# A hybrid block with two RWKV directions: the backward one put in reversed time, and triangles turned through DRAM

## The chip, the cores and the metric

The kernel runs on one core of one Trainium2 chip. The metric is the device time of one execution in microseconds (us). A core has five engines with a queue each: TensorE (PE in the profile; PEld is its loading of weights), VectorE (DVE), ScalarE (ACT), GpSimd (POOL) and SyncE (SP), which issues all of this kernel's DMAs.

## The reference

One layer of a block on 512 latent tokens and 256 context tokens of width 1024, all in f32: a projection of the normalized input into three branches (RWKV-7, convolution, mLSTM) and gates, the gated merge of the three, and an MLP. The change touches the RWKV branch alone. It has 8 heads of 64, and each of two directions runs a recurrence over the context and then over the latents; the second one runs backward in time over each:

```python
def step(S, inp):
    w_t, k_t, v_t, kk_t, a_t = inp[:5]
    S = (S * w_t[:, :, None, :]
         - jnp.einsum('bhvk,bhk->bhv', S, kk_t)[..., None] * (kk_t * a_t)[:, :, None, :]
         + v_t[..., None] * k_t[:, :, None, :])
    y = jnp.einsum('bhvk,bhk->bhv', S, inp[5]) if emit else None
    return S, y
...
for d in range(2):
    rev = d == 1
    w_c, k_c, a_c = fc[4][d]
    s_ctx, yc = _rwkv7_scan(s0, w_c, k_c, fc[2], fc[3], a_c, fc[0], rev, emit_ctx)
    w_l, k_l, a_l = fl[4][d]
    _, yl = _rwkv7_scan(s_ctx, w_l, k_l, fl[2], fl[3], a_l, fl[0], rev, True)
    y_lat = y_lat + yl
```

Decay `w` and rate `a` are the direction's own; `r`, `k`, `v` and `kk` are the same for both. The two outputs are added, normalized by head and gated.

## The kernel before, in words

Matrices lie with features on the 128 partitions and time along the free axis: 512 latent columns, then 256 of context. Dense products take every weight as a high and a low half (`whalf`, L147: a DMA of raw weights, a ScalarE copy that rounds, a POOL subtraction), three products each. The stages follow one another in program order:

- Normalization and modulation, then the feature stage: the first half of the convolution, and for the RWKV branch `shifted` (L302, a dense product and the token shift), `normalize`, `operands` (L326) and `values` (L410). `operands` works on one head and both directions at once, the forward one on partitions 0 to 63, the backward one on 64 to 127: it loads keys into `BK` and `r` into `rd` for both halves, scans the log decay within chunks of 64 (L352 forward, L353 backward with reversed operands), takes exponentials, multiplies, and stores `al` and `bk` to DRAM. `values` transposes `v` on TensorE and stores it.
- The mLSTM stage (`front` and `back` of four heads). In the middle of it stands `rw.run(rw.ctx(0), rw.lat(0))` (L482), which prepares the first pair of RWKV heads.
- Four weaves (`weave`, L1142), one for each pair of heads. A weave runs `chain(j)` (L1085): twelve chunks one after another, in each of them a product with the state (L1100), a product with the inverted triangle (L1106, operand `LT`), and the state's update (L1115 on TensorE, L1116 on VectorE). The two directions visit the chunks in different orders (`ORDER`), with their own PSUM tiles `ch0` and `ch1`, one buffer each; `u` of both goes to the lower half of `UV`, and is copied again into `UU` (L1119), from where `output` (L1072) makes one product for both directions. Between the chain's thirds (36 in a weave) the weave places other work, so much for each third by `PACE` (preparation of the next pair) and `DENSE` (products of gates and projections, some 120 in a weave); `paced` lets it issue only behind the chain's last instruction. The tail of the pair before (norm, gate) stands there too.
- Preparation of a pair is `ctx` (L922) and `lat` (L936): `gram` (L954) makes the chunks' products on TensorE and VectorE writes them masked into `LT` (L976), `LR` (L978) and the other half of `AL` (L984); `transposed` (L987) turns the keys on TensorE; `invert` (L1002) inverts the 64x64 triangles of 24 chunks. For that, VectorE transposes four blocks of 32 partitions from `LT` into `N` (L1012), so that partitions are chunks; 30 recurrence steps of two ops each (L1017, L1019) invert 32x32 triangles; two transposes make `TN` (L1022, L1024) and four take N back into `LT` (L1042); TensorE makes the off-diagonal blocks (L1033, L1034, L1048, L1049), which ScalarE copies out.
- The merge of the branches and the MLP.

The order on an engine's queue is set ahead of the run by a planner that simulates the program and takes what is ready by priority; the chain's instructions have the highest.

Of the kernel before, what the change touches and what calls it, by code (L numbers as in the profile page):

```python
# [17 lines left out]
P = 128  # L18
# [30 lines left out]
CONST_ORDER = [("ident", 128), ("bones", 128), ("gmf", 128), ("gmb", 128), ("nmf", 128), ("nmb", 128)]  # L49
# [27 lines left out]
def build(tc, wblk, wada, xin, cin, params, lora, consts, rowp, out, dbg=None):  # L77
# [45 lines left out]
    for j in range(4):  # L123
# [5 lines left out]
        sp["v", j] = DR.tile([T, P], F32, name=f"sp_v{j}")  # L129
# [164 lines left out]
    for i in range(2):  # L294
        z, y = SO.tile([P, 752], F32, name=f"z{i}"), SO.tile([P, NT], F32, name=f"cy{i}")
        gated(i, z[:, :])
        tiles.append((i, z[:, :], y[:, :]))
# [20 lines left out]
    G.memset(mk[0:64, :, 0:1], 0.0)  # L318
    G.memset(mk[64:128, :, CH - 1:CH], 0.0)

    Es = [(SO.tile([P, T], F32, name=f"E{i}"), SO.tile([P, NCH, CH], F32, name=f"Ep{i}")) for i in range(2)]
    for _, Ep in Es:
        G.memset(Ep[0:64, :, 0:1], 1.0)
        G.memset(Ep[64:128, :, CH - 1:CH], 1.0)

    def operands(j, h, kb, r):  # L326

# [27 lines left out]
        A.activation(Ep[0:64, :, 1:CH], ct[0:64, :, 0:CH - 1], AF.Exp, scale=-0.5 * RALPHA)  # L355
        A.activation(Ep[64:128, :, 0:CH - 1], ct[64:128, :, 1:CH], AF.Exp, scale=-0.5 * RALPHA)
# [5 lines left out]
        for d in range(2):  # L362
            G.tensor_copy(PL[HF[d], j, :, h:h + 1], E3[HF[d], :, CH - 1:CH] if d == 0 else E3[HF[d], :, 0:1])
# [13 lines left out]
    A.activation(wdt[:, :], t, AF.Tanh)  # L377
    t = shifted(13, True, "vj", 2)
    V.tensor_copy(adt[:, :], t)
# [30 lines left out]
    def values(j, rk):  # L410
        vj = shifted(8 + j, True, "vj", 2)
        for c2 in range(2):
            pt = PS1.tile([P, 3, P], F32, tag="tp", name="tp", bufs=1)
            for i in range(3):
                PE.transpose(pt[:, i, :], vj[:, (c2 * 3 + i) * P:(c2 * 3 + i + 1) * P], ident)
            vt = S1.tile([P, 3, P], F32, tag="vt", name="vt", bufs=2)
            A.copy(vt[:, :, :], pt[:, :, :])
            SY.dma_start(sp["v", j][c2 * 384:c2 * 384 + 384, :].rearrange("(c t) v -> t c v", t=P), vt[:, :, :])
# [7 lines left out]
    for j in range(4):  # L426
# [5 lines left out]
        rks.append(rk)  # L432
        for h in range(2):
            operands(j, h, kbs[j], rj)
# [429 lines left out]
PACE = [4] * 8 + [3] * 8 + [2] * 12 + [0] * 8  # L864
# [4 lines left out]
class Rwkv:  # L869
    ORDER = [[8, 9, 10, 11, 0, 1, 2, 3, 4, 5, 6, 7], [11, 10, 9, 8, 7, 6, 5, 4, 3, 2, 1, 0]]  # L870
# [7 lines left out]
    def pair_set(self, i, S):  # L878
        if i == 0:
            self.BK = [S.tile([P, NCH, 2, CH], F32, name=f"BK{h}") for h in range(2)]  # L880
        self.LT.append(S.tile([P, 32, CH], F32, name=f"LT{i}"))
        self.tc.nc.gpsimd.memset(self.LT[i][:, 24:32, :], 0.0)
        for h in range(2):
            for d in range(2):
                self.AL[d].append(S.tile([P, 20, CH], F32, name=f"AL{d}{i}{h}"))
            self.LR.append(S.tile([P, 8, CH], F32, name=f"LR{i}{h}"))
        if i == 0:
            self.tmp = S.tile([P, 256], F32, name="tmp")
            self.N = S.tile([P, 32, 32], F32, name="N")
            self.TN = S.tile([P, 32, 32], F32, name="TN")  # L890
# [3 lines left out]
    def open_a(self):  # L894
# [3 lines left out]
        self.PS, self.PG = PS, [PS]  # L898
        self.AL, self.LR, self.LT, self.BKt = [[], []], [], [], []
# [589 lines left out]
```

## Time and profile before

| | us |
|---|---|
| three runs | 1367.76, 1372.55, 1374.81 |
| median | 1372.55 |
| the profiled execution | 1377.12 |
| its span, first to last instruction | 1375.3 |
| TensorE matmul busy in it | 1252.9 (91%) |
| TensorE weight load busy | 969.6 (71%) |
| VectorE busy | 849.2 (62%) |
| POOL busy | 585.7 (43%) |
| ScalarE busy | 511.8 (37%) |

All stages below are read from the profiled execution, in us from the first instruction on. The stages of interest are the feature stage (its RWKV heads stand at about 160 to 272 us), the mLSTM (to 541.9) and the weaves, which begin at 541.9, 620.6, 708.4 and 796.7 us. Busy shares are means over stages of different kinds, so the rows are asked for by stretch. A matmul's busy time overlaps that of the next one. In an f32 product the records come in twos.

### The profile page before, as it was taken

How to read it: one execution, taken by the hardware profiler on the slowest of the kernel's cores; microseconds unless marked ns; L12 is line 12 of the kernel's file. 1: busy time of each engine (PE TensorE's matmuls, PEld its weight loads, DVE VectorE, ACT ScalarE, POOL GpSimd, SP SyncE). 2: the span in 40 equal slices, each digit the busy share in tenths (PEclk: the TensorE clock that was granted, in tenths of full speed). 3: DMA queues.
4: the chain of work that ended last, by engine and by line, in shares of the span. 5: the costliest groups of instructions: out<-in, count | busy, mean ns of one | idle time of the engine just before them, and what ended most of it. 6: DMA issues, size and time to landing. Idle time of an engine off the chain costs nothing.

```text
span 1375.3 us, 21700 instructions
## 1 busy us (share of the span) xinstructions
PE 1252.9 (91%) x8004; PEld 969.6 (71%) x8004; DVE 849.2 (62%) x1509; ACT 511.8 (37%) x1048; POOL 585.7 (43%) x547
## 2 busy tenths in 40 slices
PE   6999989786999886999899988889999999999997
PEld 1587877565888775667566665667888878888886
DVE  2599588889266993797977857678366534300202
ACT  4434556632222231243342444422354444322322
POOL 0443334426755441332433435533456544444442
PEclk9999999898999997999998998999999999999999
DMA  9221588732633314323431244787434433433422
GB/s 375 65 69 58 134 270 255 246 104 62 186 99 97 111 64 120 110 93 101 143 110 49 85 145 136 259 263 249 131 112 156 142 100 95 153 104 96 131 95 89
DMA packets 101457, 187.85 MB, mean 137 GB/s; under 512 B 10708, under 2 KB 29396, under 8 KB 100328
## 3 DMA queue, kind: packets, MB, share of 16 engines
q1 hardware_dynamic: 101352, 186.47, 42.9%
q8 instruction: 63, 1.03, 0.3%
q14 instruction: 42, 0.34, 0.1%
HBM read 148.64 MB, written 29.40 MB: 129 GB/s over the span
## 4 chain that ended last, share of the span: by engine, by line
PE 45%; DVE 14%; DMA 5%; issue 3%; ACT 1%; POOL 1%; SPq 0%; DVEq 0%; POOLq 0%; ACTq 0%
PE pt L1268 16%; PE pd L1337 13%; PE dg L512 5%; DMA wad<-wada 4%; DVE N L1019 3%; DVE tmp L1017 2%; PE pg L973 2%; PE ch L1100 1%; PE pd L682 1%; DVE N L1012 1%; PE ch L1106 1%; DVE accm L608 1%; PE dl L262 1%; PE pbk L998 1%; PE ch L1115 1%
## 5 line engine op out<-in xcount | busy, mean ns | idle before, releaser
L153 POOL TENSOR_TENSOR wlo<-raw,whi 128x512 fp32r<-128x512 f32 x296 | 435.5, 1477 | 555.5 <-ACT whi L152 488.9
L152 ACT CAST whi<-raw 128x512 fp32r<-128x512 f32 x296 | 182.0, 618 | 318.7 <-PE pt L1268 118.8
L262 PE MATMUL dl<-hh,wlo 128*128 128x512 f32 (+1 forms) x368 | 149.7, 407 | 10.8 <-POOL wlo L153 10.8
L262 PE MATMUL dl<-hh,whi 128*128 128x512 f32 (+1 forms) x368 | 151.4, 412 | 2.7 <-ACT kT L758 1.9
L262 PE MATMUL dl<-hl,whi 128*128 128x512 f32 (+1 forms) x368 | 148.5, 403 | 0.0
L1337 PE MATMUL pd<-h2l,whi 128*128 128x512 f32 (+1 forms) x272 | 103.3, 381 | 0.7 <-POOL h2l L1320 0.7
L1337 PE MATMUL pd<-h2h,wlo 128*128 128x512 f32 (+1 forms) x272 | 102.7, 379 | 0.0
L1337 PE MATMUL pd<-h2h,whi 128*128 128x512 f32 (+1 forms) x272 | 101.5, 380 | 0.2 <-ACT h2h L1317 0.2
L1363 DVE TENSOR_TENSOR x<-pt,modb 128x512 f32<-128x512 f32 x8 | 5.5, 690 | 154.7 <-PE pt L1268 154.7
L1268 PE MATMUL pt<-whi,h1h 128*128 128x512 f32 x256 | 99.6, 389 | 0.0
L1268 PE MATMUL pt<-whi,h1l 128*128 128x512 f32 x256 | 99.6, 389 | 0.0
L1268 PE MATMUL pt<-wlo,h1h 128*128 128x512 f32 x256 | 99.1, 389 | 0.0
L262 PEld LDWEIGHTS dl<-hh,wlo 128*128 128x128 f32 (+1 forms) x368 | 70.7, 192 | 26.0 <-POOL wlo L153 11.2
L262 PEld LDWEIGHTS dl<-hh,whi 128*128 128x128 f32 (+1 forms) x368 | 71.2, 193 | 18.6 <-ACT kT L758 2.1
L262 PEld LDWEIGHTS dl<-hl,whi 128*128 128x128 f32 (+1 forms) x368 | 70.8, 192 | 15.2 <-issue 1.5
L608 DVE SCALAR_TENSOR_TENSOR accm<-wad,sc,accm 128x512 f32<-128x512 f32 x56 | 59.1, 1056 | 35.2 <-DMA wad<-wada 34.6
L1113 POOL TENSOR_TENSOR sps<-SV,PL 64x128 f32<-64x128 f32 x88 | 40.0, 454 | 85.1 <-DVE SV L1116 81.9
L1341 DVE TENSOR_TENSOR relu<-relu 128x512 f32<-128x512 f32 x32 | 38.9, 1218 | 55.8 <-ACT relu L1340 55.7
L512 PE MATMUL dg<-hl,whi 128*128 128x512 f32 x144 | 66.5, 462 | 0.0
L512 PE MATMUL dg<-hh,whi 128*128 128x512 f32 x144 | 65.7, 456 | 0.0
L512 PE MATMUL dg<-hh,wlo 128*128 128x512 f32 x144 | 65.6, 456 | 0.0
L1019 DVE TENSOR_TENSOR N<-N,tmp 128x30 f32<-128x30 f32 (+14 forms) x120 | 58.1, 484 | 3.0
(389 smaller groups left out, 2792.3 us busy)
## 6 DMA issues: line engine op xcount, KB each, us to landing
raw<-wblk SPq DMA_DIRECT2D x296, 256.0 KB, 2.9
wad<-wada SPq DMA_DIRECT2D x64, 256.0 KB, 4.0
wada<-wada SPq DMA_DIRECT2D x8, 1024.0 KB, 13.4
BK<-kb SPq DMA_DIRECT2D x16, 384.0 KB, 5.2
sp_bk<-BK SPq DMA_DIRECT2D x8, 768.0 KB, 5.2
BK<-sp_bk SPq DMA_DIRECT2D x8, 768.0 KB, 4.1
sp_g<-gt SPq DMA_DIRECT2D x24, 256.0 KB, 2.0
sp_al<-al SPq DMA_DIRECT2D x8, 640.0 KB, 4.6
```

Source lines behind the costliest of these rows:

```text
L152: A.copy(hi[:, :], raw[:, :])
L153: G.tensor_tensor(lo[:, :], raw[:, :], hi[:, :], ALU.subtract)
L262: PE.matmul(ps_[0:M, :], lhsT=w[:, ko:ko + M], rhs=x[seg][:, k, :], start=(n == 0), stop=(n == 3 * KT - 1))
L512: yield lambda w=w, x=x, k=k, ko=ko, n=n: PE.matmul(ps[:, :], lhsT=w[:, ko:ko + P], rhs=x[:, k, :], start=(n == 0), stop=(n == 3 * KT - 1))
L608: V.scalar_tensor_tensor(o, t[:, :], sc[:, k, 0:1], o, ALU.mult, ALU.add)
L973: PE.matmul(ps[hf, i, :, :], lhsT=BK[dd, c, x, :], rhs=al[:, c] if lat else AL[d][dd, 8 + c:9 + c, :], start=True, stop=True)
L1017: V.tensor_tensor(tv, N[:, s + 1:32, s:s + 1].to_broadcast([P, n, s]), N[:, s:s + 1, 0:s].to_broadcast([P, n, s]), ALU.mult)
L1019: V.tensor_tensor(N[:, s + 1:32, 0:s], N[:, s + 1:32, 0:s], tv, ALU.add)
L1113: last["Pool"] = G.tensor_tensor(sps[hf], SV[d][hf, c, :, :], PL[hf, c, :].unsqueeze(2).to_broadcast([64, 2, CH]), ALU.mult)
L1268: PE.matmul(pss[i][:, :], lhsT=x[:, k, ts_], rhs=w[:, :], start=(k == 0 and n == 0), stop=(k == nk - 1 and n == 2))
L1337: PE.matmul(ps[:, ts_], lhsT=w[:, ko:ko + P], rhs=x[:, k, ts_], start=(k == 0 and n == 0), stop=(k == 7 and n == 2))
L1341: V.tensor_tensor(t[:, :], t[:, :], t[:, :], ALU.mult)
```

## The change

The backward direction's operands are turned round in time as they are made (each of the two segments for itself), so that in every later step it looks like the forward one.

- Feature stage: reversed copies of keys (`kr`), of `r` (`rr`) and of `v` (`vr`) on POOL, reversed writes of the two low-rank inputs; one scan over 128 partitions, one exponential for `Ep`, one copy for `PL`; `values` transposes and stores v a second time, reversed. The backward half of `bk` is stored with its two operands swapped, in runs of 64 elements. The first convolution's tiles share the tags `cw` and `rd`.
- Gram: both directions' own products lie in one PSUM tile and are masked by one VectorE op into `LT`, whose tile now holds `LR` too; the other two products keep two ops. The second tile takes the tag `m` of the same pool instead of a bank of the chain's pool.
- Inversion: `LT` is stored to DRAM and `N` is loaded from there by four DMAs in runs of 32 elements; after the recurrence, which runs from the other end over the upper triangle, N is stored and loaded back into `LT` the same way; one transpose over 128 partitions makes `TN`.
- Chain: one order, one PSUM tile with two buffers, one product by -1 for both directions; no `UU`. The output makes a product for each direction into its own PSUM tile, and the tail adds the second one, read backward.
- `PACE` gives 92 steps in a weave instead of 80.

```diff
-        sp["v", j] = DR.tile([T, P], F32, name=f"sp_v{j}")
+        for nm in ("v", "vr"):
+            sp[nm, j] = DR.tile([T, P], F32, name=f"sp_{nm}{j}")
+        sp["lt", j] = DR.tile([P, 24 * CH], F32, name=f"sp_lt{j}")
+        sp["n", j] = DR.tile([P, 1024], F32, name=f"sp_n{j}")
...
-            SY.dma_start(BK[HF[d]], kb[HF[h]])
-            SY.dma_start(rj[HF[d], :], r[HF[h], :])
+            SY.dma_start(BK[HF[d]], kb[d][HF[h]])
+            SY.dma_start(rj[HF[d], :], r[d][HF[h], :])
...
-        V.tensor_tensor_scan(ctf[0:64, :], mkf[0:64], cw[0:64, :], 0.0, ALU.mult, ALU.add)
-        V.tensor_tensor_scan(ctf[64:128, ::-1], mkf[64:128, ::-1], cw[64:128, ::-1], 0.0, ALU.mult, ALU.add)
+        V.tensor_tensor_scan(ctf, mkf, cw[:, :], 0.0, ALU.mult, ALU.add)
...
-        SY.dma_start(sp["bk", hd][:, :], BK.rearrange("p c x t -> p (c x t)"))
+        SY.dma_start(sp["bk", hd][HF[0], :], BK[HF[0]].rearrange("p c x t -> p (c x t)"))
+        for x in range(2):
+            SY.dma_start(sp["bk", hd][HF[1], :].rearrange("p (c x t) -> p c x t", x=2, t=CH)[:, :, 1 - x, :], BK[HF[1], :, x, :])
...
+        vr = S1.tile([P, NCH, 2, CH], F32, tag="kr", name="vr").rearrange("p c x t -> p (c x t)")
+        for a, z in SEG:
+            G.tensor_copy(vr[:, a:z], vj[:, a:z][:, ::-1])
...
+        kr = S1.tile([P, NCH, 2, CH], F32, tag="kr", name="kr")
+        rr = S1.tile([P, NT], F32, tag="rr", name="rr")
+        for c in (slice(0, 8), slice(8, 12)):
+            G.tensor_copy(kr[:, c], kbs[j][:, c][:, ::-1, :, ::-1])
+        G.tensor_copy(rr[:, :], rj[:, ::-1])
...
-PACE = [4] * 8 + [3] * 8 + [2] * 12 + [0] * 8
+PACE = [4] * 8 + [3] * 12 + [2] * 12 + [0] * 4
...
+            own, oth = (pool.tile([P, 4, w, CH], F32, tag=tag, name="pg") for pool, tag in ((self.PS, "g"), self.PG))
...
+            V.tensor_tensor(dst.rearrange("p x c t -> p c x t"), own[:, :, :, :], mo, ALU.mult)
+            yield
             for d in range(2):
...
+                V.tensor_tensor(dst, oth[od], mx[od], ALU.mult)
                 yield
...
-        for q in range(4):
-            d, bl = q // 2, q % 2
-            qs = slice(32 * q, 32 * q + 32)
-            src = LT[qs, :, 32 * bl:32 * bl + 32].rearrange("p g t -> p t g")
-            V.transpose(N[qs] if d == 0 else N[qs].rearrange("p a b -> p b a"), src)
-            yield
-        for s in range(1, 31):
+        lt, n_ = self.sp["lt", j], self.sp["n", j]
+        Q = [(32 * (q % 2), slice(32 * q, 32 * q + 32), slice(32 * q, 32 * q + 24)) for q in range(4)]
+        SY.dma_start(lt[:, :], LT.rearrange("p g t -> p (g t)"))
+        for o, qs, qg in Q:
+            SY.dma_start(N[qg], lt[qs, :].rearrange("s (g t) -> g s t", t=CH)[:, :, o:o + 32])
+        yield
+
+        for _ in range(2):
+            yield from tr
+            for _ in range(4):
+                yield
+        for s in range(30, 0, -1):
...
         G.memset(N.rearrange("p a b -> p (a b)")[:, 0:1024:33], 1.0)
-        V.transpose(TN[0:32].rearrange("p g s -> p s g"), N[0:32].rearrange("p t s -> p s t"))
+        SY.dma_start(n_[:, :], N.rearrange("p a b -> p (a b)"))
+        for o, qs, qg in Q:
+            SY.dma_start(LT[qs, :, o:o + 32], n_[qg, :].rearrange("g (s t) -> s g t", t=32))
+        V.transpose(TN.rearrange("p g s -> p s g"), N[:, :, :])
         yield
-        V.transpose(TN[96:128].rearrange("p g s -> p s g"), N[96:128])
-        yield
...
-        for q in range(4):
-            d, bl = q // 2, q % 2
-            qs = slice(32 * q, 32 * q + 32)
-            src = N[qs] if d == 0 else N[qs].rearrange("p a b -> p b a")
-            V.transpose(LT[qs, :, 32 * bl:32 * bl + 32].rearrange("p g t -> p t g"), src)
+        for _ in range(6):
             yield
...
-                for d in range(2):
-                    PE.matmul(o, lhsT=self.SV[d][:, c, h, :], rhs=self.AL[d][sl[h]][:, c, :], start=(d == 0), stop=False)
-                PE.matmul(o, lhsT=self.UU[:, c, h, :], rhs=self.LR[sl[h]][:, c, :], start=False, stop=True)
+                    o = py[d][HF[h], c * CH:(c + 1) * CH]
+                    PE.matmul(o, lhsT=SV[d][:, c, h, :], rhs=self.AL[d][sl[h]][:, c, :], start=True, stop=False)
+                    PE.matmul(o, lhsT=UV[d][HF[d], c, h, :], rhs=LR[HF[d], h * 12 + c, :], start=False, stop=True)
...
-            chs = [PS.tile([P, 3, 2, CH], F32, tag=f"ch{d}", name=f"ch{d}") for d in range(2)]
+            ch = PS.tile([P, 3, 2, CH], F32, tag="ch", name="ch", bufs=2)
...
-            for d, c, ch, hf in zip(range(2), cs, chs, HF):
-                if c < 8:
-                    last["ACT"] = A.copy(self.UU[hf, c, :, :], ch[HF[0], 1])
...
-        A.copy(y[:, :], self.py[:, :])
+        A.copy(y[:, :], self.py[0][:, :])
+        V.tensor_tensor(y[:, :], y[:, :], self.py[1][:, ::-1], ALU.add)
```

## Rows read from the trace of the kernel before

**Rows 1.** stages; stretch, PE, PEld, DVE, ACT, POOL busy (count), clock, DMA, GB/s

```profile
160.00:272.00 112.00, 99.02 (x469) 76.64 (x467) 94.64 (x91) 68.51 (x107) 47.51 (x38) 0.96 0.84 247
...
440.00:541.90 101.90, 81.07 (x600) 67.84 (x599) 83.32 (x215) 23.90 (x45) 39.22 (x43) 0.92 0.30 94
...
620.60:708.40 87.80, 79.64 (x948) 56.57 (x947) 73.69 (x143) 33.16 (x97) 31.41 (x44) 0.92 0.34 105
```

**Rows 2.** timeline of PE: start, us, engine, line, op, tiles, shapes, count

```profile
628.50 0.73 PE L1106 MATMUL ch<-xc,LT 64*64 64x64 f32 x4
...
715.69 0.32 PE L1106 MATMUL ch<-xc,LT 64*64 64x64 f32 x2
```

**Rows 3.** four stretches from 628.5 to 715.7, columns as in rows 1

```profile
628.50:650.20 21.70, 21.29 (x221) 14.79 (x217) 12.11 (x28) 6.31 (x18) 7.02 (x9) 0.84 0.22 66
...
650.20:664.40 14.20, 11.26 (x92) 8.05 (x93) 12.40 (x17) 3.44 (x10) 3.52 (x6) 0.76 0.36 118
...
664.40:701.00 36.60, 32.77 (x321) 22.30 (x322) 34.10 (x92) 15.64 (x50) 16.43 (x22) 1.00 0.35 107
...
701.00:715.70 14.70, 13.72 (x287) 10.49 (x285) 12.65 (x8) 7.91 (x21) 2.45 (x5) 1.00 0.35 108
```

**Rows 4.** timeline of DVE, PE, SP; in brackets idle time before, its releaser

```profile
501.25 8.54 DVE L1042 STREAM_TRANSPOSE LT<-N 32x1024 f32<-32x1024 f32 x4
...
650.23 4.29 DVE L1012 STREAM_TRANSPOSE N<-LT 32x1024 f32<-32x1024 f32 x2
...
655.29 0.69 DVE L984 TENSOR_TENSOR AL<-pg,cst 64x512 f32<-64x512 f32 x1
...
656.13 1.97 PE L973 MATMUL pg<-AL,BK 64*64 64x128 f32 x16 [2.94 <-DVE AL L984]
...
662.61 1.25 SPq L1067 DMA_DIRECT2D UV<-sp_v  x2
```

**Rows 5.** waits of PE, 541.9 to 880: who <- releaser: us, times, longest

```profile
PE ch L1100 <- ACT UU L1119: 12.7, 19, 1.8
...
PE pg L973 <- DVE AL L984: 8.5, 3, 3.1
```

**Rows 6.** groups by line, DVE: count | busy us, mean ns | idle before

```profile
L1012 DVE STREAM_TRANSPOSE N<-LT 32x1024 f32<-32x1024 f32 x16 | 32.3, 2017 | 0.2
...
L1042 DVE STREAM_TRANSPOSE LT<-N 32x1024 f32<-32x1024 f32 x16 | 32.6, 2038 | 0.4
...
L976 DVE TENSOR_TENSOR LT<-pg,cst 64x256 f32<-64x256 f32 x48 | 20.2, 421 | 47.6 <-PE pg L973 47.1
```

**Rows 7.** groups by line, ACT and PE, columns as in rows 6

```profile
L1119 ACT COPY UU<-ch 64x128 f32<-64x128 f32 x64 | 16.5, 258 | 43.0 <-DVE SV L1116 41.7
...
L1081 PE MATMUL py<-AL,SV 128*64 128x64 f32 x256 | 19.6, 233 | 0.0
...
L1082 PE MATMUL py<-LR,UU 128*64 128x64 f32 x128 | 15.4, 231 | 0.0
```

**Rows 8.** DMA issues: out<-in, engine, op, count, KB each, median us to landing

```profile
sp_bk<-BK SPq DMA_DIRECT2D x8, 768.0 KB, 5.2
...
UV<-sp_v SPq DMA_DIRECT2D x24, 128.0 KB, 3.1
...
sp_v<-vt SPq DMA_DIRECT2D x8, 192.0 KB, 4.4
...
sp_gd<-gtt SPq DMA_DIRECT2D x4, 256.0 KB, 2.0
```

**Rows 9.** groups by line, feature stage and mLSTM, as in rows 6

```profile
L353 DVE TENSOR_TENSOR_SCAN ct<-scm,cw 64x768 f32<-64x768 bf16 x8 | 17.7, 2213 | 0.2
...
L415 PE MATMUL tp<-cst,vj 128*128 128x128 f32 x24 | 4.9, 314 | 1.4 <-DVE bo L422 0.8 <-ACT vt L417 0.6
...
L778 POOL TENSOR_SCALAR to<-to 128x512 f32<-128x512 f32 x4 | 6.1, 1522 | 0.0
```

**Rows 10.** waits of PE, 440 to 541.9, columns as in rows 5

```profile
PE pt L856 <- DVE ht L855: 7.6, 2, 6.1
```

More of the change, by code (lines that the diff above doesn't have):

```diff
@@ L411, in values @@
         vj = shifted(8 + j, True, "vj", 2)
[L412 to L418, printed above, removed]
+        vr = S1.tile([P, NCH, 2, CH], F32, tag="kr", name="vr").rearrange("p c x t -> p (c x t)")
+        for a, z in SEG:
+            G.tensor_copy(vr[:, a:z], vj[:, a:z][:, ::-1])
+        for nm, vx in (("v", vj), ("vr", vr)):
+            for c2 in range(2):
+                pt = PS1.tile([P, 3, P], F32, tag="tp", name="tp", bufs=1)
+                for i in range(3):
+                    PE.transpose(pt[:, i, :], vx[:, (c2 * 3 + i) * P:(c2 * 3 + i + 1) * P], ident)
+                vt = S1.tile([P, 3, P], F32, tag="vt", name="vt", bufs=2)
+                A.copy(vt[:, :, :], pt[:, :, :])
+                SY.dma_start(sp[nm, j][c2 * 384:c2 * 384 + 384, :].rearrange("(c t) v -> t c v", t=P), vt[:, :, :])
         pl = PS1.tile([P, NT], F32, tag="tp", name="hs", bufs=1)
@@ L919, in head @@
         sl = (2 * j + h) % 4
-        return [self.AL[d][sl] for d in range(2)], self.LR[sl], self.BKt[sl], self.bk[j, h]
+        return [self.AL[d][sl] for d in range(2)], self.BKt[sl], self.bk[j, h]
     def ctx(self, j):
@@ L945, in lat @@
             yield from self.gram(j, h, (0, 1))
-        tr = self.flat(self.transposed(j, h, (0, 1)) for h in range(2))
-        for i, _ in enumerate(self.invert(j)):
-            yield
-            if i % 8 == 7:
-                next(tr, None)
-                yield
-        yield from tr
+        yield from self.invert(j, self.flat(self.transposed(j, h, (0, 1)) for h in range(2)))
     def gram(self, j, h, quarters):
@@ new lines, in gram @@
+            lat = c4 < 2
+            w = 2 if lat else 1
+            own, oth = (pool.tile([P, 4, w, CH], F32, tag=tag, name="pg") for pool, tag in ((self.PS, "g"), self.PG))
+            for i in range(4):
+                c = c4 * 4 + i
+                for x, ps in enumerate((own, oth)):
+                    for d in range(2):
+                        dd, hf = HF[d], HF[(d + x) % 2]
+                        al = AL[d][dd, 0:16, :].rearrange("p (x c) t -> p c x t", x=2)[:, c] if lat else AL[d][dd, 8 + c:9 + c, :]
+                        PE.matmul(ps[hf, i, :, :], lhsT=BK[dd, c, (d + x) % 2, :], rhs=al, start=True, stop=True)
@@ L1068, in load @@
             if c4 == 2:
                 for d in range(2):
[L1070 removed]
+                    G.memset(SV[d][HF[d], self.ORDER[0], :, :], 0.0)
     def output(self, j):
[L1074 removed]
+        PE, HF = self.tc.nc.tensor, self.HF
         sl = [(2 * j + h) % 4 for h in range(2)]
[L1076 to L1077 removed]
+        SV, UV, LR = self.SV, self.UV, self.LT[j % 2][:, 1]
```

152 lines of the change are left out of this document (67 added, 85 removed).

## The prediction

> **What bounds the kernel now.** I read the busy time by stage first, then the stretch that repeats, then its waits. In the stages by stretch [rows 1] TensorE is the fullest engine, but it isn't full in any of them: in the mLSTM stretch it is busy 81.1 of 101.9 us, in a weave (one pair's chain with the next pair's inversion beside it) 79.6 of 87.8 us. The granted clock is 0.92 there, so 8% of a weave, 7 us, is lost to TensorE's lower level (1.2 GHz, half of 2.4). VectorE comes next (83.3 of 101.9, 73.7 of 87.8). In the feature stage (160 to 272 us) the limits lie side by side: TensorE 99.0 of 112, VectorE 94.6, DMA 0.84 of the time.
>
> What sets the length of a weave? The first product with the inverted triangle (L1106) of the second weave starts at 628.5 us and that of the third at 715.7, 87.2 us later [rows 2], though the third weave itself had begun at 708.4. It waits for its triangle. So the inversion for the next pair is a loop of its own as long as the weave, and [rows 3] cuts it in four: 21.7 us in which the gram products of the next pair are made (TensorE 21.3 busy), 14.2 us of transposes into N with the last gram evictions (VectorE 12.4 busy), 36.6 us of recurrence (VectorE 34.1 busy), 14.7 us of transposes out, the 32-wide products and the copies (VectorE 12.7 busy). In the last three, 65.5 us, VectorE is the engine that ends last. The stretch of the transposes in is also where TensorE stands: it waits 2.94 us for AL, whose eviction is queued behind a 4.29 us pair of transposes, and the clock of that stretch is 0.76 [rows 3, 4]. Three such waits make 8.5 us in the weaves, and 19 waits for the copy into UU make 12.7 us [rows 5].
>
> **Off VectorE.** Per pair four transposes in (16 x 2.02 us in all) and four out (16 x 2.04) go, and the two into TN, of the same 32x1024 form, become one over 128 partitions with the same 1024 elements each, so again 2.0 us: per pair 20.3 us become 2.0, over four pairs -73 us [rows 6]. Gram: per quarter of latent chunks 2 x (0.42 + 0.42 + 0.69) = 3.06 us (the LR op is of LT's shape) become three of AL's 0.69, 2.07 us; 16 quarters give -16 us, and the 8 of context chunks -3 us (four ops of 0.42 become three) [rows 4, 6]. In the feature stage the scan of 64 partitions backward (17.7 us in 8) goes into the one forward [rows 9]. The tail gains one 128x512 op from PSUM, 4 x 0.7 us. The 60 recurrence steps per pair keep their shapes. Sum about -107 us of 849, of which only what lies in the loop or before a waiting TensorE counts.
>
> **Off and onto the other engines.** ScalarE loses the 64 copies into UU (16.5 us) [rows 7] and half of the 96 products by -1. What they free is the wait of L1100; the next in line is the state's add on VectorE just before, so I take half of the 12.7 us. TensorE gains: the output's third product, once for both directions, is made twice; 128 records cost 15.4 us, so 64 more instructions cost up to 15.4 and, by the neighbouring line (19.6 us for 256), 10 us: 2.5 per weave [rows 7]. 24 more transposes of values cost 4.9 us, as the 24 now do [rows 9]. POOL gains the reversed copies: 2048 elements a pair for keys and r, 768 for v. No row shows a reversed copy; the nearest is 1.52 us for 512 elements [rows 9], so up to 33 us in all, and not below zero. POOL is busy 47.5 of 112 us there [rows 1], so it has room; queued behind are the low halves of the weights, for which TensorE waits.
>
> **Through DRAM.** Each inversion gets two round trips, one store and four loads each, in runs of 128 bytes. The trace has no such run, so both ends: the store is 768 KB, and the store of that size lands in 5.2 us; the loads are 96 KB each, four behind one another at 0.62 us of issue (1.25 for two [rows 4]), the last landing 3.1 us after (128 KB in runs of 512 bytes). That is 5.2 + 1.9 + 3.1 = 10.2 us at best. At worst each run costs what it does in the 192 KB store of 512-byte runs: (4.4 - 2.0) us for 384 runs, 6.3 ns a run, 3072 runs 19 us, so 5.2 + 2 + 19 = 26 us [rows 8]. I take 13: nearer the best, since that row is a DMA of nearly the same size, plus 3 us for SP. SP issues in order: the loads wait there for the store's landing, with weight loads (L149) queued behind, and may themselves queue behind a gate's store (L517) that waits for its gate. Weight loads fall due every 9 us or so (12 products to a half, some 120 in a weave), which covers one 13 us wait badly and a second one not.
>
> First the row: 16 transposes into N cost 2.02 us each, 8 us a pair, less than my best DMA leg of 10.2 [rows 6, 8]. The Trainium skill, page "VectorE: DVE Perf Modes", section "Rules for kernel authors", says that for a 32x32 transpose within a bank VectorE's own is the fastest; by that rule each leg gets longer and the result is the first rival's. The row agrees as to the leg; it says nothing on what the engine does meanwhile.
>
> **The loop, new.** While the second round trip runs, VectorE is free for the gram of the next pair, which now starts some 8 us after the weave does (at 628.5 instead of 620.6), and its evictions are shorter: 21.7 becomes 15. Round trip in 13; recurrence 36.6 becomes 34 (2.5 us of it is not VectorE's); round trip out 13, with TN and the first 32-wide products inside it; second products and copies 2. Sum 77 us against 87.5. TensorE's own work is then next: 79.6 busy, +2.5 output, less half of the 7 us of clock, 78.6. Neither is met without gaps; I take 80.5, -7 us for each of three weaves, -21. The last weave has no inversion: half its UU wait (-2) against output and tail (+3): 0, bounds -4 to +4.
>
> **mLSTM stretch.** The first inversion runs here. 16 us of transposes leave VectorE (eight of 2.0 us [rows 6]), which delay the mLSTM's own ops: TensorE waits 7.6 us for ht [rows 10]. The last transposes out end at 509.8 us [rows 4], 32 us before the first weave, which hides the two round trips; without that cover they cost the rival's price. I take -8; bounds -15 (all of that wait and some clock) and +5.
>
> **Feature stage.** TensorE +4.9 us beside -17.7 us on VectorE, and DMA: half of each bk store goes in runs of 256 bytes, 1536 a head, by the 6.3 ns above up to 9.7 us instead of 2.6; at best nothing more. Eight heads in 112 us with DMA at 0.84 leave 18 us of cover. The reversed copy also stands before BK's second load. I take +5, bounds -5 and +25.
>
> **Rivals.** (1) The round trips decide: the loop is 15 + 34 + 2 + twice the trip, and above 18 us a trip it is longer than today's 87.5. At 22 us, inside the bounds, it is 95: +7.5 x 3 = 22, with mLSTM -5 and features +5, 1394 us. For it: the short runs, SP's order, the missing 128-byte row. Against it: DMA is only 0.34 busy in a weave [rows 1]. (2) The feature stage takes it back: DMA or the reversed copies end last there, +25 instead of +5, 1369 us, no change. For it: 0.84 DMA. Against it: VectorE's relief. (3) The weave is TensorE's and not the inversion's: the loop shortens, TensorE doesn't, and only waits of 8.5 us and their clock go: -10 instead of -21, 1360. (4) A 128-partition transpose is paid by quarter, 8.4 us instead of 2.1: 6 us a pair, inside the round trip, so hidden.
>
> **How the numbers follow.** The profiled execution is 1377.1 us (span 1375.3); the median of the runs is 1372.6, 4.6 less. 1377.1 - 21 - 8 + 5 = 1353, less 4.6: 1349. Its own range: -30 (10 per weave, TensorE's own work at full clock), -15, -5 give 1323; weaves -10, mLSTM 0, features +5 give 1367. Chances: forecast with (3) and (4) 0.62, rival (2) 0.17, rival (1) 0.21. A measurement tells 0.5%, 7 us, from no change: faster is under 1366, which holds the forecast, 0.62; same 0.17; slower 0.21. The range goes from 1323 to 1395, which takes in (2) and half of (1).
>
> **What would show it.** Right: no TensorE wait for AL in the weaves, VectorE busy under 55 of some 81 us, first triangle products 80 us apart, and the wait for UU gone. Wrong in the trips: VectorE idle for several us ahead of the first recurrence step or TensorE ahead of L1048's successor, waiting for a DMA. Wrong in the features: bk stores landing later than 7 us and the head's period above 13 us.

## The result and the profile after

The changed kernel takes 1476.55 us (median of four runs, 1467.99 to 1480.52) against 1373.2 us: a ratio of 1.073 (95% interval 1.068 to 1.078). The forecast was 1349 us and faster. Of the four executions of the fourth experiment's kernel below, two took 1496 us at a granted clock of 0.90 where the others had 0.93, and its time is given by the others alone. The profiled execution of the changed kernel has a span of 1472.7 us, 97.4 more than before. By the first and the last products of the chains (the first line's stretch lies inside the second's):

| us | before | after | difference |
|---|---|---|---|
| gates of the mLSTM turned (last input's first product) | 315.8 | 343.8 | +28.0 |
| first weave begins | 541.9 | 552.8 | +10.9 |
| from there to the last triangle product of the chains | 341.9 | 429.7 | +87.8 |
| rest (merge, MLP) | 491.5 | 490.2 | -1.3 |

So the loss lies in the four weaves, where the forecast had its gain of 21 us. The stretches of the changed kernel, one for each weave (columns as in rows 1: stretch, PE, PEld, DVE, ACT, POOL busy, granted clock, DMA share, GB/s):

```profile
552.80:641.80 89.00, 78.33 (x847) 54.75 (x849) 42.40 (x103) 21.90 (x57) 25.68 (x38) 0.86 0.42 119
641.80:744.00 102.20, 94.47 (x873) 66.77 (x871) 45.87 (x116) 25.66 (x64) 31.84 (x43) 0.91 0.40 116
744.00:860.10 116.10, 107.49 (x1058) 75.13 (x1056) 45.89 (x118) 29.17 (x72) 31.48 (x43) 0.81 0.29 83
860.10:982.50 122.40, 106.64 (x610) 70.93 (x608) 55.64 (x107) 34.17 (x78) 45.30 (x44) 0.74 0.49 151
```

Against [rows 1] two things have changed. VectorE, busy 73.7 us in the second weave before, is busy 45.9 there. And the clock, 0.89 to 0.92 in the four weaves before, is 0.81 and 0.74 in the last two, while TensorE is busy for 107 of 116 us in the third. VectorE has in fact got rid of what the forecast took off it: 849.2 us of the whole span became 742.0, as its sum of 107 us had it. What TensorE has got instead stands in the groups by line (count | busy us, mean ns | idle before), with some of the smaller terms:

```profile
L1093 PE MATMUL py<-AL,SV 128*64 128x64 f32 x256 | 47.9, 276 | 0.0
...
L1094 PE MATMUL py<-LT,UV 64*64 64x64 f32 x256 | 47.6, 273 | 0.0
...
L1038 DVE STREAM_TRANSPOSE TN<-N 128x1024 f32<-128x1024 f32 x4 | 8.0, 2009 | 0.3
...
L356 DVE TENSOR_TENSOR_SCAN ct<-scm,cw 128x768 f32<-128x768 bf16 x8 | 14.2, 1776 | 0.9 <-ACT cw L353 0.9
...
L448 POOL COPY kr<-kb 128x1024 f32<-128x1024 f32 (+1 forms) x8 | 11.6, 1479 | 19.3 <-DMA BK<-kr 10.0 <-DMA raw<-wblk 7.7 <-DVE kb L416 1.6
...
L422 POOL COPY vr<-vj 128x512 f32<-128x512 f32 (+1 forms) x8 | 9.3, 1189 | 14.6 <-DVE cy L294 12.7 <-DMA BK<-kr 1.0 <-POOL vr L422 0.9
```

The output's two lines stood at 19.6 us for 256 products' records and 15.4 us for 128 [rows 7]; now they stand at 47.9 and 47.6, 60 us more, where the forecast had 10. Records come in twos, so it is 256 products. And in TensorE's waits (total us, times, longest) a new one has come first:

```profile
PE ch L1127 <- DVE SV L1128: 24.5, 23, 5.0
...
PE pg L979 <- DVE AL L992: 2.7, 3, 1.2
```

The wait for UU [rows 5] is gone, and the wait of 8.5 us for AL [rows 5] is down to 2.7. But the second direction's products with BKt (L1127) now wait 24.5 us for SV, which VectorE adds up (L1128) for the first direction.

### The profile page after: what moved, and what is told of

Same layout as the page of the kernel before. It is cut to its first block, busy times and chain, and to the rows that moved or that the text cites. A ratio compares the mean times of both kernels' runs of the same rounds, so it can differ in the third digit from the quotient of the medians.

```text
span 1472.7 us, 21884 instructions
## 1 busy us (share of the span) xinstructions
PE 1343.0 (91%) x8156; PEld 1028.0 (70%) x8156; DVE 742.0 (50%) x1415; ACT 487.0 (33%) x938; POOL 580.6 (39%) x555
## 4 chain that ended last, share of the span: by engine, by line
PE 59%; DVE 8%; DMA 7%; issue 1%; SPq 1%; ACT 1%; POOL 0%; DVEq 0%; ACTq 0%; POOLq 0%
PE pt L1278 15%; PE pd L1347 12%; PE dg L529 7%; PE dl L265 5%; DMA wad<-wada 3%; PE py L1093 3%; PE py L1094 3%; PE pg L979 2%; PE dp L608 2%; PE ch L1127 2%; DVE tmp L1030 2%; PE pd L699 1%; DVE N L1032 1%; PE dc L265 1%; DMA N<-sp_lt 1%
## 5 line engine op out<-in xcount | busy, mean ns | idle before, releaser
L156 POOL TENSOR_TENSOR wlo<-raw,whi 128x512 fp32r<-128x512 f32 x296 | 404.5, 1370 | 545.7 <-ACT whi L155 502.7
L1128 DVE TENSOR_TENSOR SV<-ch,sps 64x128 f32<-64x128 f32 x88 | 25.3, 288 | 120.5 <-PE ch L1127 86.5
L529 PE MATMUL dg<-hh,whi 128*128 128x512 f32 x144 | 70.6, 490 | 0.0
L529 PE MATMUL dg<-hl,whi 128*128 128x512 f32 x144 | 70.5, 490 | 0.0
L1351 DVE TENSOR_TENSOR relu<-relu 128x512 f32<-128x512 f32 x32 | 42.9, 1341 | 54.2 <-ACT relu L1350 54.2
L529 PE MATMUL dg<-hh,wlo 128*128 128x512 f32 x144 | 69.8, 485 | 0.0
L1127 PE MATMUL ch<-UV,BKt 128*64 128x64 f32 x352 | 44.6, 258 | 24.8 <-DVE SV L1128 24.5
```

What stands on the lines that cost most here:

```text
L156: G.tensor_tensor(lo[:, :], raw[:, :], hi[:, :], ALU.subtract)
L529: yield lambda w=w, x=x, k=k, ko=ko, n=n: PE.matmul(ps[:, :], lhsT=w[:, ko:ko + P], rhs=x[:, k, :], start=(n == 0), stop=(n == 3 * KT - 1))
L1127: last["PE"] = PE.matmul(ch[hf, 2, h, :], lhsT=BKt[h][:, c, hf], rhs=UV[d][:, c, h, :], start=True, stop=True)
L1351: V.tensor_tensor(t[:, :], t[:, :], t[:, :], ALU.mult)
```

## Where the time went: two readings of the trace

**Theory A, the tile's shape.** The timeline of TensorE (start, us, line, tiles, rows*columns of the array in use) in the second weave's output:

```profile
744.39 0.33 PE L1094 MATMUL py<-LT,UV 64*64 64x64 f32 x2
744.64 0.33 PE L1093 MATMUL py<-AL,SV 128*64 128x64 f32 x2
744.90 0.33 PE L1094 MATMUL py<-LT,UV 64*64 64x64 f32 x2
```

Each row is one product (two records). A product with the state uses 128 rows, the one with u 64 rows, because u of one direction fills 64 partitions; they alternate, and each starts 0.255 us after the one before, at a granted clock of 1.00. Among its like a product takes less. The mean durations of [rows 7] don't show that, since records overlap; the distance of the starts does, in the third experiment's kernel, where the same products are grouped by shape:

```profile
768.17 0.46 PE L1093 MATMUL py<-AL,SV 128*64 128x64 f32 x8
...
768.55 0.34 PE L1097 MATMUL py<-LT,UV 64*64 64x64 f32 x8
...
768.83 0.46 PE L1093 MATMUL py<-AL,SV 128*64 128x64 f32 x8
```

Four products of one shape start 0.38 us (128 rows) and 0.28 us (64 rows) ahead of the next group, 0.66 us for eight and not 8 x 0.255 = 2.04. The eight still hold two changes of shape and not eight, so six changes cost 1.38 us, 0.23 us each; what products of one shape gain by running side by side is in that. For 32 chunks the alternation costs 32 x 1.38 = 44 us at full clock.

The Trainium skill, page "TensorEngine Tiling (Array Packing)", section "Key Properties", says that changing the tiling mode, not just the tile, drains TensorE. The trace agrees in that a change costs time, those 0.23 us here; it doesn't show the draining itself.

The clock is low in two stretches where this happens, with the output of the third and of the fourth weave (columns as above):

```profile
828.80:872.00 43.20, 42.73 (x326) 29.81 (x325) 1.15 (x4) 7.09 (x21) 4.13 (x6) 0.59 0.16 40
...
945.00:987.00 42.00, 41.05 (x200) 28.02 (x200) 13.57 (x19) 8.69 (x20) 12.39 (x12) 0.51 0.48 156
```

TensorE's records fill these stretches nearly whole (42.73 of 43.2 us, 41.05 of 42), and yet the granted clock is 0.59 and 0.51, for most of the time the lower of its two levels (1.2 of 2.4 GHz). The busy share alone doesn't show it. The same alternation stands in the output of the first two weaves (620 to 658 and 721.9 to 754.1 us), and there the clock is 0.91 and 0.95: the alternation alone doesn't bring it down.

**Theory B, one tile for both directions.** In the changed chain both directions' results lie in one PSUM tile. The program multiplies for direction 0, adds on VectorE, multiplies for direction 1, adds. Rows of SP, VectorE and TensorE around 691 us, in that order:

```profile
680.50 0.33 SPq L1018 DMA_DIRECT2D sp_lt<-LT  x1
...
685.60 2.30 SPq L1020 DMA_DIRECT2D N<-sp_lt  x4
...
691.65 0.20 DVE L1030 TENSOR_TENSOR tmp<-N 128x30 f32<-128x30 f32 x1 [3.37 <-DMA N<-sp_lt]
...
693.39 0.28 DVE L1128 TENSOR_TENSOR SV<-ch,sps 64x128 f32<-64x128 f32 x1
...
690.60 0.45 PE L1127 MATMUL ch<-UV,BKt 128*64 128x64 f32 x4
...
693.72 0.37 PE L1127 MATMUL ch<-UV,BKt 128*64 128x64 f32 x1 [2.68 <-DVE SV L1128]
```

The store of LT goes out at 680.50 us, the loads of N at 685.60, and VectorE stands for 3.37 us before its first recurrence step. Direction 0's products (690.60, four records) are long done, but their addition (693.39) stands in VectorE's queue behind that step; and direction 1's products, of the same kind, start 2.68 us late behind the addition, since it reads the tile that they write to. Before, each direction had its own tile. Such waits do a second thing: they cut the eight records of a chunk into four and four, with other products between them where the planner finds some (64x64 and 128x128 ones at 665 us).

**Theory C, the round trips** (the forecast's first rival) and **theory D**, for the feature stage, stand with their experiments below.

## The experiments

Ratios go by the kernel before on the same chip; "weaves" is the time from the first weave's first product to the chains' last triangle product.

| kernel | median us | ratio (95% interval) | weaves us |
|---|---|---|---|
| before | 1373.2 | 1 | 341.9 |
| after | 1476.55 | 1.0729 (1.0683 to 1.0776) | 429.7 |
| 1 output in groups of a shape | 1417.51 | 1.0304 (1.0241 to 1.0367) | 380.2 |
| 2 additions behind both directions' products | 1412.24 | 1.0287 (1.0225 to 1.0349) | 360.5 |
| 3 both | 1368.21 | 0.9974 (0.9945 to 1.0003) | 320.5 |
| 4 after, N by VectorE again | 1460.65 | 1.0632 (1.0551 to 1.0712) | 417.3 |
| 5 both, a tile of its own for vr | 1355.41 | 0.9868 (0.9820 to 0.9915) | 321.5 |
| 6 before, with shape changes | 1378.73 | 1.0051 (1.0023 to 1.0079) | 343.8 |
| 7 both, N by VectorE again | 1378.14 | 1.0033 (1.0002 to 1.0064) | 331.9 |
| 8 both, the old pace | 1367.6 | 0.9972 (0.9946 to 0.9999) | 318.2 |
| 9 both, values reversed by TensorE | 1358.83 | 0.9863 (0.9822 to 0.9904) | 320.8 |
| 10 as 5, all of bk in short runs | 1362.85 | 0.9894 (0.9845 to 0.9942) | 322.0 |
| 11 as 5, the second trip longer | 1369.77 | 0.9950 (0.9922 to 0.9978) | 334.6 |

### 1. Output in groups

```diff
             for h in range(2):
                 for d in range(2):
                     o = py[d][HF[h], c * CH:(c + 1) * CH]
                     PE.matmul(o, lhsT=SV[d][:, c, h, :], ..., start=True, stop=False)
+            for h in range(2):
+                for d in range(2):
+                    o = py[d][HF[h], c * CH:(c + 1) * CH]
                     PE.matmul(o, lhsT=UV[d][HF[d], c, h, :], ..., start=False, stop=True)
```

> The output's products of a chunk are made in two groups, four with the state (128 rows) and then four with u (64 rows), so that the tile's shape changes twice in a chunk and not eight times; nothing else differs. Theory A (shape changes): an alternating product takes 0.257 us to the next at full clock where one among its like takes 0.107, so 32 chunks x 6 changes x 0.15 = 29 us at full clock and some 35 at the granted one, and the clock of the last two weaves (0.78 and 0.74) comes back to about 0.9, another 15 to 40 us: 1476 becomes 1400 to 1425. Theory B (one PSUM tile for both directions, so that the second direction's state products stand behind the first one's addition) and theory C (round trips through DRAM): within 10 us of 1476, since neither is touched.

Measured 1417.51 us, 59 less. The two lines' groups, the chain's wait, and the last weave:

```profile
L1093 PE MATMUL py<-AL,SV 128*64 128x64 f32 x256 | 19.1, 252 | 0.0
...
L1097 PE MATMUL py<-LT,UV 64*64 64x64 f32 x256 | 14.4, 261 | 0.0
...
PE ch L1130 <- DVE SV L1131: 26.2, 24, 3.7
...
829.70:936.00 106.30, 87.39 (x606) 57.97 (x603) 61.17 (x109) 34.47 (x78) 44.63 (x44) 0.79 0.57 178
```

The output's lines fall from 95.5 to 33.5 us; that is theory A's. The wait of theory B is untouched (26.2 us, 24 times), and the last weave still has a clock of 0.79.

### 2. Additions behind both directions' products

```diff
                     for h in range(2):
                         last["PE"] = PE.matmul(ch[hf, 2, h, :], lhsT=BKt[h][:, c, hf], rhs=UV[d][:, c, h, :], ...)
+                for d, hf in enumerate(HF):
                     last["DVE"] = V.tensor_tensor(SV[d][hf, cn, :, :], ch[hf, 2], sps[hf], ALU.add)
```

> In the chain the state products of both directions are issued ahead of the two additions on VectorE, so that the second direction's products no longer wait for the first one's addition, which reads the same PSUM tile. Theory B: the 24.5 us of TensorE's waits for SV before these products go, and a few us of the half clock behind them: 1440 to 1455. Theory A or C alone: within 10 us of 1476, since TensorE would be filled by other work as now.

Measured 1412.24 us, 64 less and well below what theory B had been given. The wait, the output's line and the last weave:

```profile
PE ch L1110 <- DVE SV L1129: 10.8, 10, 2.4
...
L1093 PE MATMUL py<-AL,SV 128*64 128x64 f32 x256 | 43.9, 256 | 0.0
...
808.30:913.50 105.20, 98.89 (x790) 67.61 (x786) 54.08 (x97) 35.38 (x82) 42.57 (x44) 0.79 0.49 154
```

The wait of L1127 is gone, and what is left of it stands at the next chunk's first product (10.8 us). The output still costs what it did. The gain is more than twice the wait, and rows show two things beside it. The eight records of a chunk stand together again; the products of L1127 (L1115 in the kernel before) had taken twice their time in the changed kernel (before, after, this kernel):

```profile
L1115 PE MATMUL ch<-UV,BKt 128*64 128x64 f32 x352 | 22.1, 244 | 2.2 <-ACT UV L1109 2.2
...
L1127 PE MATMUL ch<-UV,BKt 128*64 128x64 f32 x352 | 44.6, 258 | 24.8 <-DVE SV L1128 24.5 <-ACT UV L1119 0.2
...
L1127 PE MATMUL ch<-UV,BKt 128*64 128x64 f32 x352 | 21.4, 245 | 2.3 <-ACT UV L1119 2.3
```

And the clock of the first two weaves is 0.95 and 0.98 where it was 0.86 and 0.91. How the 64 us divide among the wait, these products and the clock isn't shown, since the one edit touches all three. In the last weave, with the output's alternation still there, the clock stays at 0.79.

### 3. Both

> Both edits in one kernel: output products in groups of one shape, and the additions behind both directions' products. Theories A and B together: the gains add, some 35 + 25 us and the clock behind both, 1370 to 1400, with the granted clock of the four weaves at 0.9 or above. Theory C: still above 1440.

Measured 1368.21 us, 108 less; the weaves take 320.5 us, 21.4 less than in the kernel before, where the forecast had 21. The four weaves, columns as above:

```profile
548.30:610.70 62.40, 59.53 (x667) 40.58 (x669) 37.57 (x88) 17.83 (x49) 24.88 (x37) 0.94 0.54 157
610.70:694.50 83.80, 78.01 (x963) 55.43 (x960) 52.80 (x123) 27.66 (x68) 31.33 (x43) 0.92 0.49 139
694.50:779.00 84.50, 77.27 (x962) 54.80 (x958) 49.20 (x121) 27.37 (x68) 31.54 (x43) 0.94 0.41 113
779.00:868.60 89.60, 80.91 (x788) 54.44 (x784) 56.15 (x101) 35.13 (x82) 43.09 (x45) 0.89 0.54 169
```

The clock is back at 0.89 to 0.94, which neither edit alone brought about in the last weave (0.79 both times). The two gains add up to a little less than their sum (59 + 64 = 123).

### 4. The round trip into N undone

```diff
-        SY.dma_start(lt[:, :], LT.rearrange("p g t -> p (g t)"))
-        for o, qs, qg in Q:
-            SY.dma_start(N[qg], lt[qs, :].rearrange("s (g t) -> g s t", t=CH)[:, :, o:o + 32])
-        yield
+        LX = self.LT[j % 2].rearrange("p x g t -> p (x g) t")[:, 0:32]
+        for o, qs, qg in Q:
+            V.transpose(N[qs].rearrange("p a b -> p b a"), LX[qs, :, o:o + 32].rearrange("p g t -> p t g"))
+            yield
```

> The first of the two round trips of each inversion is undone: N comes from four VectorE transposes as in the kernel before (about 8 us of VectorE a pair), the second trip stays. Theory C (the trips set the loop): the weaves shorten by the trip less the transposes; a trip takes some 10 us from the store to the first recurrence step, so about 2 us a weave at most, and 20 us and more only if the trips cost more than they show: 1440 to 1470. Theories A and B: TensorE sets the weave and VectorE is busy 45 of 102 us, so nothing: 1466 to 1486.

Measured 1460.65 us, 16 less than the changed kernel by the medians and 13 by the ratios, whose intervals meet; it lies in theory C's range and just under that of A and B. The weaves say that it isn't the trip's own time: of the three with an inversion the first two take 5.8 and 4.2 us longer than in the changed kernel and the third 15.1 us less, at a clock of 0.93 and not 0.81; the last, which has no inversion, takes 7.3 us less. So most of the loss stays without the trip into N, and what the trip is worth is left to the seventh experiment. A wait of TensorE comes back with the transposes (first row), each of which takes 1.9 us (second row, two of them):

```profile
PE pbk L1006 <- DVE AL L992: 19.3, 3, 7.2
...
589.78 3.82 DVE L1020 STREAM_TRANSPOSE N<-LT 32x1024 f32<-32x1024 f32 x2
```

### 5. A tile of its own for the reversed values

```diff
-        vr = S1.tile([P, NCH, 2, CH], F32, tag="kr", name="vr").rearrange("p c x t -> p (c x t)")
+        vr = S1.tile([P, T], F32, tag="vr", name="vr")
```

> On top of both chain edits of the third run, the reversed copy vr gets a tile of its own instead of the one buffer that it shares with the reversed keys kr. Theory D (the shared buffer holds the values back until the last head's keys are loaded, so that their products start at 265 us and not at 230 and the mLSTM's gates some 23 us late): the last product for the bonus ends near 275 to 290 instead of 306 us, and the end comes 5 to 15 us earlier, 1353 to 1363. Rival (the feature stage is bound by DMA, busy 0.9 of the time, and what it loses the mLSTM stage gives back anyway): within 4 us of 1368.

Measured 1355.41 us, with an interval that doesn't meet the third run's: faster than both kernels, by 1.3% of the one before. Each pair of rows is after, then this kernel; up to the reversed keys the two profiles run level (their first copy starts at 166.5 and 166.6 us), while the third kernel's is 4 us ahead by then (162.5). The first pair is the gates turned for the mLSTM (L768), the second the product for the bonus (L432), with first and last start:

```profile
L768 PE MATMUL tp<-cst,b x6: 297/298/318, 343.8 to 345.2; 36*128 36x36 f32 x6
...
L768 PE MATMUL tp<-cst,b x6: 298/298/320, 333.1 to 334.5; 36*128 36x36 f32 x6
```

```profile
L432 PE MATMUL hs<-rk,cst x8: 592/826/1222, 265.5 to 311.4; 128*128 128x512 f32 x8
...
L432 PE MATMUL hs<-rk,cst x8: 591/826/1221, 240.2 to 300.0; 128*128 128x512 f32 x8
```

The bonus begins 25 us earlier, since the values no longer wait for the buffer of the last head's keys, but its last product moves by 11 us alone (300.0, not the 275 to 290 expected), and the gates by 10.7. The seven kernels with the shared buffer have the gates at 338.5 to 346.2 us, the four with another arrangement of vr at 332.9 to 334.9. They are still 17 us behind the kernel before (315.8). What holds these 17 us wasn't found; the mLSTM stage gives nearly all of them back, since the first weave begins at 543.9 us, 2.0 behind.

### 6. Shape changes in the kernel before

```diff
-                for d in range(2):
-                    PE.matmul(o, lhsT=self.SV[d][:, c, h, :], rhs=self.AL[d][sl[h]][:, c, :], start=(d == 0), stop=False)
+                PE.matmul(o, lhsT=self.SV[0][:, c, h, :], rhs=self.AL[0][sl[h]][:, c, :], start=True, stop=False)
+                for q in (slice(0, 32), slice(32, 64)):
+                    PE.matmul(o[q], lhsT=self.SV[1][:, c, h, q], rhs=self.AL[1][sl[h]][:, c, :], start=False, stop=False)
```

> The kernel before with one thing changed: of the three output products of a chunk and head the second is made as two products of 32 output partitions each, in the middle, so that the tile's shape goes from 128x64 to 128x32 and back; 64 chunks and heads get one product and two shape changes more. Theory A (a shape change costs some 0.15 us at full clock, whatever the shapes): 64 x 0.107 = 7 us for the products and 128 x 0.15 = 19 us for the changes, with the clock behind them 20 to 40 us: 1392 to 1412. Rival (only the number of rows, or the mix with the second direction's tile, costs): the products alone, 1376 to 1384.

Measured 1378.73 us, 0.5% more, which is the rival's number and not theory A's. But the rows speak for A: one product of 128x64 ahead of two of 128x32 takes 0.26 us (605.10 to 605.36), though the number of rows is the same, and the output's busy time goes from 35.0 [rows 7] to 60.7 us, 512 records in place of 384 at 1.7 times the busy time:

```profile
L1080 PE MATMUL py<-AL,SV 128*64 128x64 f32 x128 | 20.6, 243 | 0.0
...
L1082 PE MATMUL py<-AL,SV 128*32 128x64 f32 x256 | 19.7, 233 | 0.0
...
L1083 PE MATMUL py<-LR,UU 128*64 128x64 f32 x128 | 20.4, 241 | 0.0
...
605.10 0.33 PE L1080 MATMUL py<-AL,SV 128*64 128x64 f32 x2
...
605.36 0.31 PE L1082 MATMUL py<-AL,SV 128*32 128x64 f32 x4
```

So a change of the columns costs as a change of the rows does. In time it costs little here, and the granted clock of the last three weaves, 0.94 to 0.96, is no lower than before (0.90 to 0.92): changes of shape alone, at this number, don't bring the clock down. That TensorE has room in weaves that wait for their triangle would explain the first three; it wasn't tested, and the last weave, which prepares no triangle, got no longer either. What was wrong in the expectation is the step from busy time to time.

### 7. The round trip into N undone, with the chain cured

> On top of both chain edits of the third run, the round trip into N is undone again (four VectorE transposes as in the kernel before). With the chain cured the weave waits for its triangle again (the first triangle products stand about 80 us apart), so here the trip's worth should show. The forecast's loop: 8 us of VectorE instead of a trip of about 10 us, and VectorE then stands in the way of the gram's evictions: between 3 us faster and 6 us slower a weave, 1358 to 1386. Theory C (the trips set the time): 1345 or less.

The edit of the fourth experiment on top of the third. Measured 1378.14 us, 10 more than with the trip by the medians and 8 by the ratios (whose intervals just touch); the weaves take 11.4 us longer. In them, one wait of TensorE has come back:

```profile
PE pg L979 <- DVE AL L992: 15.2, 3, 5.4
```

It is the wait for AL's eviction behind the transposes that the forecast wanted gone [rows 4, 5]. So the trip through DRAM is worth 8 to 10 us once the chain doesn't hide it, though it takes longer than the transposes it stands for.

### 8. The old pace

> On top of both chain edits, the old pace of the preparation: 80 steps in the 36 thirds of a weave instead of 92, the rest behind the chain. If the new pace is what keeps TensorE filled: the preparation's last steps go behind the chain and the next triangle comes later, 2 to 5 us a weave, 1374 to 1384. If the pace doesn't decide: within 4 us of 1368.

`PACE` as before, on top of both edits: 1367.6 us. The pace doesn't decide.

### 9. Values reversed on TensorE

In place of `vr` and its transposes, the transposed values are multiplied by a permutation that reverses 128 rows, and stored as the reversed ones:

```diff
-            G.tensor_copy(vr[:, a:z], vj[:, a:z][:, ::-1])
...
+            PE.matmul(pt[:, :, :], lhsT=J[:, :], rhs=vt[:, ::-1, :], start=True, stop=True)
```

> On top of both chain edits, the reversed copy vr and its 24 transposes go: the values, transposed once, are multiplied on TensorE with a reversing permutation (8 products in place of 24 transposes), so that nothing of the values shares a buffer with kr or waits for POOL. Theory D (the values were held back by the reversed copy's buffer): at least the gain of the own tile, 1345 to 1358. Rival (the feature stage ends with DMA or VectorE in any case): the same as with the own tile, 1352 to 1360, or as without, 1368, if the longer chain from transpose to product costs what it saves.

Measured 1358.83 us, a ratio of 0.986 where the own tile has 0.987: the same. So neither POOL's copies of v nor the 24 added transposes cost; the shared buffer did. The copies of the keys and of r stand in both kernels, and no run takes them out.

### 10. Short runs doubled

```diff
-        SY.dma_start(sp["bk", hd][HF[0], :], BK[HF[0]].rearrange("p c x t -> p (c x t)"))
+        for x in range(2):
+            SY.dma_start(sp["bk", hd][HF[0], :].rearrange("p (c x t) -> p c x t", x=2, t=CH)[:, :, x, :], BK[HF[0], :, x, :])
```

> On top of both chain edits and the own tile for vr, the forward half of bk is stored in runs of 256 bytes too (two DMAs of half the size in place of one), so that the suspected cost of the short runs in the feature stage is doubled. By the forecast's bounds: nothing at best, 9.7 - 2.6 us a head at worst, of which 18 us lie under cover: 1353 to 1395; if the short runs are what holds the feature stage back, 10 us and more over 1355; if the shared buffer was, within 4 us of it.

A ratio of 0.989 (0.985 to 0.994) where the fifth has 0.987: 3.6 us by the ratios (7.4 by the medians), inside the intervals. The gates come at 334.9 us where the fifth has 333.1. The runs of 256 bytes are not what holds the feature stage back.

### 11. A longer second trip

```diff
         SY.dma_start(n_[:, :], N.rearrange("p a b -> p (a b)"))
+        n2 = self.sp["n2", j]
+        SY.dma_start(n2[:, :], n_[:, :])
+        n_ = n2
```

> On top of both chain edits and the own tile for vr, the second round trip is made longer: N is copied once more from DRAM to DRAM before it is loaded back, about 5 us more from the store to the loads. If the inversion's loop still sets the weave (forecast): 4 to 5 us for each of three weaves, 1367 to 1372, the first weave's trip being under cover. If TensorE's own work sets it (the forecast's third rival): 1353 to 1359.

Measured 1369.77 us, 14 more by the medians and 11 by the ratios; the weaves take 13.1 us longer. TensorE now waits for the loads:

```profile
PE px L1062 <- DMA LT<-sp_nn: 13.2, 3, 8.4
```

So with the chain cured the inversion's loop sets the weave, as the forecast had it, and not TensorE's own work.

## Why the prediction was wrong, step by step

- **TensorE's added products: the step that failed first.** The forecast priced 64 more output products by the neighbouring line of [rows 7], 10 to 15 us in all. That is a price of products among their like, where it was even too high: in groups, in the third kernel, all 256 take 27.4 us (15.1 and 12.3), less than the 35.0 of the 192 before. The new product uses 64 rows of the array beside one of 128, and the order alternates them. Busy time grew by 60 us, and the first experiment gets 59 us of time back. The diff and the 64x64 form of L1106 in [rows 2] were there to see that two forms would stand in turn.
- **The chain's one tile: a step that wasn't there.** "One PSUM tile with two buffers" stood in the change, and the forecast gave it no line. It is a wait added, of direction 1's products on direction 0's addition, and VectorE's queue stands ahead of that addition: 24.5 us of wait, 64 us of time by the second experiment, which also puts the chain's records together again.
- **The loop and VectorE's relief: right in the end, under the other two, and in part by luck.** 107 us came off VectorE, the priced terms about as priced (the scan over 128 partitions takes 1.78 us, no longer than one of 64 did [rows 9]). With both causes cured the weaves fall by 21.4 us (21 in the forecast), though the one profile of the kernel before is 4.6 us above its median, so that a few of these may be its own; the wait for AL is 0.3 us; VectorE is busy 49 to 53 of 84 us in the two middle weaves; and the first triangle products stand 79.9 and 84.0 us apart (80 in the forecast). The timeline of the fifth kernel, between the first two the start of each part of the loop:

```profile
626.15 0.44 PE L1119 MATMUL ch<-xc,LT 64*64 64x64 f32 x2
...
649.74 0.33 SPq L1018 DMA_DIRECT2D sp_lt<-LT  x1
...
660.81 0.20 DVE L1030 TENSOR_TENSOR tmp<-N 128x30 f32<-128x30 f32 x1 [3.02 <-DMA N<-sp_lt]
...
694.94 0.33 SPq L1035 DMA_DIRECT2D sp_n<-N  x1
...
704.34 0.21 PE L1058 MATMUL px<-LT,TN 32*32 32x32 f32 x1
...
706.00 0.33 PE L1119 MATMUL ch<-xc,LT 64*64 64x64 f32 x2
...
789.96 0.33 PE L1119 MATMUL ch<-xc,LT 64*64 64x64 f32 x4
```

  Gram, trip in, recurrence, trip out and the rest take 23.6, 11.1, 34.1, 9.4 and 1.7 us, where the forecast had 15, 13, 34, 13 and 2. The gram was put 8.6 us too short: it doesn't begin inside the second trip but behind the first triangle products (its first product starts at 626.3). The trips were put 5.5 us too long. The two errors nearly cancel, and that is luck. (The 87.5 us that the forecast's sum starts from are 87.2 in its own rows.)
- **The round trips: the sign was the first rival's, its mechanism wasn't.** From the store of LT to the first recurrence step it takes 8.6 to 11.2 us in the four inversions of the changed kernel (680.50 to 691.65 in the rows above), from the store of N to the first product that reads LT again 8.8 to 14.6, where the forecast took 13 between 10.2 and 26: nearer its best end. The first rival's 1394 us needed 22. The forecast's own sign of a wrong trip did show, VectorE idle ahead of the first recurrence step, for 1.8 to 5.0 us in the four, and yet the trips aren't what costs: the seventh experiment takes the first one out and loses 8 to 10 us. No run takes out the second. As to the rule of the Trainium skill that the forecast weighed (page "VectorE: DVE Perf Modes", section "Rules for kernel authors"), the transposes are indeed the faster leg, 8 us against some 10, and still the slower kernel. The fourth rival falls too: the transpose over 128 partitions takes 2.0 us (L1038), not 8.4.
- **Feature stage: +5 forecast, +28 at its end.** It is about the second rival's time (+25), and neither of its mechanisms is borne out. POOL's reversed copies take some 26 us (the two lines shown and 4.9 us for r; 33 at most in the forecast), and those of v do no harm, nor do the short runs. The eight heads run to time: the last scan starts at 255.6 us, at 257.3 before, and bk stores land 3.7 and 5.0 us after issue in the fifth kernel, 5.2 before [rows 8], under the 7 that would have shown the forecast wrong. The loss comes with the values behind them: the last product for the bonus starts at 311.4 us and not at 273.6. Some 11 us of it are the one buffer shared by kr and vr; 17 stay open.
- **mLSTM stage: -8 forecast.** From the gates to the first weave it takes 209.0 us and not 226.1: 17.1 less, beyond the bound of 15. Much of what the feature stage loses is given back here, so the two terms hang together, and the sum of both (+10.9, with the own tile +2.0) is what should have been forecast.
- **Last weave: 0 forecast.** 89.8 us before, 89.6 with both causes cured, both from the first direction's first product (794.0 before; 796.7 is the second direction's).

Why the clock fell in the last two weaves, and not in the output of the first two, isn't settled: each edit alone leaves the last weave at 0.79, both bring 0.89.

## What to carry to other kernels

Price a product on TensorE with its neighbours: note the rows and columns of the array that each product of an inner loop uses, count the changes, and issue like beside like. Where a change lets two chains share a tile, or a buffer, look for who reads it in between, and what is queued ahead of that reader; it costs a line in the sum even where the diff only drops a tag. And when an engine is relieved of 107 us, the next bound may be neither the second of before nor a wait that was listed, but one that the change itself has made.

## What the runs showed that was not expected

- A product that changes the tile's shape starts 0.255 us after the one before, at full clock, and four in a row of the same shape take 0.28 to 0.38 us in all, the change behind them included; the 0.26 us came between 128x64 and 64x64 and between 128x64 and 128x32.
- TensorE's records can fill a stretch (41.05 of 42 us) while the granted clock is 0.51: the busy share doesn't tell whether the clock holds.
- A round trip through DRAM with 768 KB out and four loads of 96 KB in runs of 128 bytes takes 8.6 to 11.2 us to the first use, about what the nearest rows gave at their best (10.2).
